# Output projection by Strassen's seven products, with the mixed heads stored in the forms the products use

## The chip, the cores and the metric

The kernel runs on one core of a Trainium2 chip. The core has five engines that run side by side, each through its own queue in order: TensorE (PE in the profile, with its weight loads as PEld), VectorE (DVE), ScalarE (ACT), GpSimd (POOL) and SyncE (SP, which here only issues DMAs). The metric is the device time of one execution in microseconds (us), taken as the median of several runs.

## The reference

One layer of a hybrid decoder, for 512 tokens and a model width of 2048, all in float32. A projection of the normalised and modulated input feeds a state space branch (SSD) and a retention branch. Their outputs, 2048 columns each, are laid side by side, and one output projection brings the 4096 columns back to 2048:

```
mixed = jnp.concatenate([y_ssd, y_ret], axis=-1) @ w_out[layer]
h = h + gate[:, None, :] * mixed
return rms_norm(h, final_norm_w)
```

The change concerns the product `@ w_out` (512 x 4096 by 4096 x 2048), what comes after it, and the place where the two branches hand over their outputs.

## The kernel before, in words

**Every float32 product is three products.** The matrices are split into a high part of reduced precision and the rest: ACT casts (`hi`, L96; `mh`, L655), DVE subtracts (`lo`, L97; `ml`, L656). `mm3` (L104 to L106) then issues high by high, high by low and low by high into the same bank of PSUM. One matmul has 128 rows of contraction, 128 output rows and 512 output columns.

**Input projection.** `unit` computes 512 columns at a time: for each of 8 steps `load_w` brings 256 rows of weights (512 KB) through SP into one of three buffers with the tag `raw`, splits them, and PE makes 24 matmuls. Units for the state space groups come first (`xs1` to `xs3`, `z1` to `z3`), then for each of four pairs of retention heads `qk`, `v` and `g`. Beside `v`, `gate_part` loads the weights of the residual gate through the same three `raw` buffers and multiplies them on DVE (L527, L529).

**Handover.** `ssd_b` and `ret_c` end in four calls of `put_mix(i, src, nw)`. It transposes a 512 x 128 block on PE, scales it on ACT into `m` (L331), and POOL sends it to DRAM as `mix[i]`, 128 features by 512 tokens (L332). There are 32 such blocks.

**Output projection.** For each of four blocks of 512 output columns there are 16 steps `kc`. A step reads two blocks `mix` (POOL's queue, L639, into the tag `xs`; blocks 12 to 31 are read once and stay in SBUF) and 256 rows of `w_out` (SP's queue), splits both, and makes 24 matmuls into four banks, one for each block of 128 tokens (tile `o`). Then for each of the four: times the gate (`h<-o,gate`, L680), plus the residual (L681), the squares' sum for the last norm on ACT (`jk`, L683), times the norm's weight (L686). In the last block of columns the four last steps are held back and PE takes them token block by token block, in an order written out by hand, so that a row of outputs can be finished and sent while PE works on the next (L689 to L699).

**Order.** The order of the instructions on each engine is set when the kernel is compiled: a planner runs through the program with costs of its own and puts each instruction where it thinks it ready, in the order of the program among equals. On the chip each queue then keeps that order, and an instruction that waits holds up all behind it on its engine. Buffers with the same tag take turns: the fourth `raw` waits until the first is free. `hi` and `lo` have four buffers each, `ul` (where `mh` and `ml` lie) has 17.

Of the kernel before, what the change touches and what calls it, by code (L numbers as in the profile page):

```python
# [41 lines left out]
def hybrid_block(ctx, tc, x, c_row, vecs, heads, w_mod, w_gate, b_gate, w_in, w_dt, w_out, fnw,  # L42
# [35 lines left out]
    # silu(c), halved conv taps and norm weights (the gates below carry a factor 2)  # L78
# [23 lines left out]
    def mm3(dst, a, b, first, last):  # L102
        (ah, al), (bh, bl) = a, b
        pe.matmul(dst, lhsT=ah, rhs=bh, start=first, stop=False)  # L104
        pe.matmul(dst, lhsT=ah, rhs=bl, start=False, stop=False)  # L105
        pe.matmul(dst, lhsT=al, rhs=bh, start=False, stop=last)  # L106
# [211 lines left out]
    mix = [dram.tile([P, L], F32, name=f"mix{i}") for i in range(32)]  # L318
# [6 lines left out]

    def put_mix(i, src, nw):
# [4 lines left out]
        act.activation(m, pT, AF.Copy, scale=nw)  # L331
        pool.dma_start(mix[i], m)  # L332

# [1 line left out]
    def ssd_a(g):  # L335
# [15 lines left out]
        for c in range(NC):  # L351
# [29 lines left out]
            if c < NC - 1:  # L381
                xw = t2k("xw", 1, "xw")
                pool.tensor_tensor(v8(xw), v8(xd), bcast_h(dte[:, c, hs]), ALU.mult)
                pst = bank("aux", "pst")
                pe.matmul(pst, lhsT=bn[:, sl], rhs=xw, start=True, stop=True)
                new = t2k("prev", 2, "new")
                if c == 0:
                    act.copy(new, pst)
                else:
                    pool.tensor_tensor(v8(new), v8(prev), bcast_h(cdec[:, c, hs]), ALU.mult)  # L390
                    dve.tensor_tensor(new, pst, new, ALU.add)
                prev = new
# [31 lines left out]
    def ret_a(p, qk):  # L424
        rr = [rotary(qk[i], f"r{i}") for i in range(4)]
        sts, kzs, qxs = [], [], []
        for j in range(2):
# [8 lines left out]
            for c in range(NC):  # L436
# [5 lines left out]
                              dmk[:, h, :].unsqueeze(1).to_broadcast([P, NC, P]), ALU.mult)  # L442
# [3 lines left out]
                               xib[:, h, :].unsqueeze(1).to_broadcast([P, NC - 1, P]), ALU.mult)  # L446
# [93 lines left out]
    dts = t2k("mo", 2, "dts")  # L540
# [52 lines left out]
    acsT = t2k("mo", 2, "acsT", (P, P))  # L593
# [36 lines left out]
    kept = {}  # L630

    def mix_tile(k):
        if k in kept:
            return kept[k]
        if k < RING:
            mr = t2k("xs", 5, "mr")
        else:
            kept[k] = mr = res.tile([P, L], F32, tag=f"mix{k}", name=f"mr{k}")
        pool.dma_start(mr, mix[k])  # L639
        return mr  # L640

    sso = const.tile([P, NC, 4], F32, name="sso")
    hout = [[None] * 4 for _ in range(NC)]
    for n in range(4):
        cols = slice(n * 512, (n + 1) * 512)
        banks = [bank("mm", f"o{t}") for t in range(NC)]
        fw = t2k("bc", 5, f"fw{n}")
        sp.dma_start(fw, fnw[cols].partition_broadcast(P))
        for kc in range(16):
            mh, ml = [], []  # L650
            for kt in range(2):
                mr = mix_tile(2 * kc + kt)
                mhk = up.tile([P, L], F32R, tag="ul", bufs=NK + 1, name="mh")
                mlk = up.tile([P, L], F32R, tag="ul", bufs=NK + 1, name="ml")
                act.copy(mhk, mr)  # L655
                dve.tensor_tensor(mlk, mr, mhk.bitcast(F32), ALU.subtract)  # L656
                mh.append(mhk)
                ml.append(mlk)
            hi, lo = load_w(w_out[16 * n + kc], 512)
            tail = n == 3 and kc >= 12  # L660
            if kc <= 12 or not tail:
                held = []
            held.append((kc, mh, ml, hi, lo))
            if tail and kc < 15:
                continue
            order = [(e, b, kt) for e in held for kt in range(2) for b in range(NC)]
            if tail:
                order = [(e, b, kt) for b in range(NC) for e in held for kt in range(2)]
            ctl = tc.manual_schedule(engines={pe.engine}) if tail else nullcontext()
            ctl.__enter__()  # L670
            for (kc_, mh_, ml_, hi_, lo_), b, kt in order:
                sl = slice(b * P, (b + 1) * P)
                mm3(banks[b], (mh_[kt][:, sl], ml_[kt][:, sl]), (hi_[:, kt, :], lo_[:, kt, :]),
                    kc_ == 0 and kt == 0, kc_ == 15 and kt == 1)
            ctl.__exit__(None, None, None)
        for t in range(NC):
            xr = t2k("zs", 4, "xr")
            sp.dma_start(xr, x[t * P:(t + 1) * P, cols])
            h = up.tile([P, 512], F32, tag="uh", bufs=NK, name=f"h{t}_{n}")
            dve.tensor_tensor(h, banks[t], gate[n], ALU.mult)  # L680
            dve.tensor_tensor(h, h, xr, ALU.add)  # L681
            jk = res.tile([P, 512], F32, tag="jk", bufs=2, name="jk")
            act.activation(jk, h, AF.Square, accum_out=sso[:, t, n:n + 1])  # L683
            hout[t][n] = h
            if n < 3:
                dve.tensor_tensor(h, h, fw, ALU.mult)  # L686
                continue
            rs = small.tile([P, 1], F32, name="rs")
            dve.tensor_reduce(rs, sso[:, t, :], mybir.AxisListType.X, ALU.add)  # L689
            rsqrt_into(rs, rs, 1.0 / D, EPS)  # L690
            for m in range(4):
                h = hout[t][m]
                if m == 3:
                    dve.scalar_tensor_tensor(h, h, rs, fw, ALU.mult, ALU.mult)
                elif m == 2:
                    dve.tensor_scalar(h, h, rs, None, ALU.mult)
                else:
                    act.activation(h, h, AF.Copy, scale=rs)
                (sp if m % 2 else act).dma_start(out[t * P:(t + 1) * P, m * 512:(m + 1) * 512], h)  # L699
# [74 lines left out]
```

## Time and profile before

| | |
|---|---|
| median of 3 runs | 1522.89 us (1522.87 to 1524.67) |
| span of the profiled execution, first to last instruction | 1520.7 us |
| what the median has beyond that span | 2.2 us |
| busy, share of the span: PE, DVE, ACT, POOL | 97%, 57%, 35%, 18% |
| output projection, first to last matmul | 1161.1 to 1510.9 us, 1536 matmuls |
| moved by DMA | 228.65 MB, 150 GB/s over the span |

The profiled execution's time is known by its span alone; it lies 2.2 us under the median, and the difference is what stands around the first and the last instruction. "Busy" is the time in which at least one instruction of the engine ran. Matmuls overlap in the pipeline, so PE's pace is read from the distance of their starts and not from the length of one. A row of the timeline gives start and length; where an instruction had to wait inside the engine, its length contains that wait.

### The profile page before, as it was taken

Reading aid. Unit: us, or ns where it says so; the run is one execution under the profiler, and the core shown is the slowest. Engines: PE = TensorE matmul, PEld = TensorE weight load, DVE = VectorE, ACT = ScalarE, POOL = GpSimd, SP = SyncE. Lnnn points to the kernel's source line nnn. Section 1 sums busy time; section 2 is a strip of 40 time slices with the busy share of each in tenths; the row PEclk is TensorE's granted clock in tenths of the full one; section 3 lists DMA queues with packets and bytes.
Section 4 is the critical chain, followed back from the end, with each engine's and each line's share of the span. In section 5 each row is a group of like instructions: output and inputs, shape, how many; then the busy total and the mean of one; then the engine's idle time right before and its main releaser. Section 6 shows DMA issues by size and latency. Waiting matters only on the chain.

```text
span 1520.7 us, 17260 instructions
## 1 busy us (share of the span) xinstructions
PE 1473.2 (97%) x6673; PEld 1205.0 (79%) x6673; DVE 861.4 (57%) x1080; ACT 531.4 (35%) x744; POOL 275.8 (18%) x326
## 2 busy tenths in 40 slices
PE   6998999999999999999999999999999999999997
PEld 4766888778888888788878887888788888888886
DVE  6899777774554563733364345435444455464644
ACT  6423443534323433122222221222223444444443
POOL 4540015360042041200020011002021310000000
PEclk9999999999999999999999999999999999999999
DMA  9888542434234224522452345234546754463523
GB/s 358 330 311 278 171 126 84 138 112 124 86 110 135 87 84 152 165 92 85 142 182 70 97 152 173 69 95 148 188 125 193 254 157 159 121 189 95 173 93 111
DMA packets 63060, 228.65 MB, mean 150 GB/s; under 512 B 7809, under 2 KB 7985, under 8 KB 58881
## 3 DMA queue, kind: packets, MB, share of 16 engines
q1 hardware_dynamic: 50834, 188.89, 38.5%
q0 software_dynamic: 10992, 36.56, 7.1%
q10 hardware_dynamic: 1152, 2.10, 0.4%
q8 instruction: 52, 0.85, 0.2%
q14 instruction: 30, 0.25, 0.0%
HBM read 214.87 MB, written 12.65 MB: 150 GB/s over the span
## 4 chain that ended last, share of the span: by engine, by line
PE 69%; DVE 6%; DMA 5%; POOL 2%; issue 1%; ACT 1%; ACTq 0%; POOLq 0%; DVEq 0%
PE acc L105 14%; PE acc L106 14%; PE acc L104 14%; PE o L106 8%; PE o L104 8%; PE o L105 8%; DMA graw<-w_gate_d 4%; DVE lo L97 2%; PE py L372 1%; PE po L466 1%; PE pT L329 1%; DVE gacc L529 1%; PE po L468 1%; PE pkv L487 1%; POOL r L421 1%
## 5 line engine op out<-in xcount | busy, mean ns | idle before, releaser
L97 DVE TENSOR_TENSOR lo<-raw,hi 128x1024 fp32r<-128x1024 f32 x230 | 285.8, 1244 | 295.9 <-ACT hi L96 295.4
L96 ACT CAST hi<-raw 128x1024 fp32r<-128x1024 f32 x248 | 254.0, 1027 | 564.1 <-PE acc L106 241.9
L104 PE MATMUL acc<-hi,uh 128*128 128x512 f32 x704 | 274.6, 393 | 6.6 <-DVE rt L420 6.3
L105 PE MATMUL acc<-lo,uh 128*128 128x512 f32 x704 | 278.7, 396 | 0.0
L106 PE MATMUL acc<-hi,ul 128*128 128x512 f32 x704 | 276.4, 393 | 0.0
L106 PE MATMUL acc<-uh,lo 128*128 128x512 f32 x512 | 200.9, 393 | 0.0
L105 PE MATMUL acc<-ul,hi 128*128 128x512 f32 x512 | 200.6, 392 | 0.0
L104 PE MATMUL acc<-uh,hi 128*128 128x512 f32 x512 | 200.4, 393 | 0.0
L104 PE MATMUL o<-hi,mh 128*128 128x512 f32 x512 | 199.4, 389 | 0.0
L105 PE MATMUL o<-lo,mh 128*128 128x512 f32 x512 | 199.3, 389 | 0.0
L106 PE MATMUL o<-hi,ml 128*128 128x512 f32 x512 | 197.7, 389 | 0.0
L104 PEld LDWEIGHTS acc<-hi,uh 128*128 128x128 f32 x704 | 132.2, 188 | 35.2 <-DVE rt L420 7.5
L656 DVE TENSOR_TENSOR ml<-mr,mh 128x512 fp32r<-128x512 f32 x128 | 88.4, 692 | 125.5 <-PE o L105 98.1
L106 PEld LDWEIGHTS acc<-hi,ul 128*128 128x128 f32 x704 | 132.3, 188 | 27.4 <-issue 0.5
L105 PEld LDWEIGHTS acc<-lo,uh 128*128 128x128 f32 x704 | 132.3, 188 | 27.2 <-issue 0.5
L105 PEld LDWEIGHTS acc<-ul,hi 128*128 128x128 f32 x512 | 96.6, 189 | 19.8
L104 PEld LDWEIGHTS acc<-uh,hi 128*128 128x128 f32 x512 | 96.6, 189 | 19.5
L106 PEld LDWEIGHTS acc<-uh,lo 128*128 128x128 f32 x512 | 96.5, 188 | 19.7
L105 PEld LDWEIGHTS o<-lo,mh 128*128 128x128 f32 x512 | 96.1, 188 | 20.0
L106 PEld LDWEIGHTS o<-hi,ml 128*128 128x128 f32 x512 | 96.1, 188 | 19.9
L104 PEld LDWEIGHTS o<-hi,mh 128*128 128x128 f32 x512 | 96.1, 188 | 19.7
L655 ACT CAST mh<-mr 128x512 fp32r<-128x512 f32 x128 | 79.1, 619 | 70.2 <-PE o L106 62.9
(220 smaller groups left out, 1668.5 us busy)
## 6 DMA issues: line engine op xcount, KB each, us to landing
ada<-w_mod_d SPq DMA_DIRECT2D x32, 1024.0 KB, 5.8
raw<-w_out_d SPq DMA_DIRECT2D x64, 512.0 KB, 3.7
mr<-mix POOLq DMA_DIRECT2D x68, 256.0 KB, 3.8
raw<-w_in_z SPq DMA_DIRECT2D x32, 512.0 KB, 3.6
raw<-w_in_qk SPq DMA_DIRECT2D x32, 512.0 KB, 3.6
raw<-w_in_v SPq DMA_DIRECT2D x32, 512.0 KB, 3.8
graw<-w_gate_d SPq DMA_DIRECT2D x32, 512.0 KB, 4.2
raw<-w_in_g SPq DMA_DIRECT2D x32, 512.0 KB, 3.6
```

Of the source, the lines that this page charges most:

```text
L96: act.copy(hi, raw)
L97: eng.tensor_tensor(lo, raw, hi.bitcast(F32), ALU.subtract)
L104: pe.matmul(dst, lhsT=ah, rhs=bh, start=first, stop=False)
L105: pe.matmul(dst, lhsT=ah, rhs=bl, start=False, stop=False)
L106: pe.matmul(dst, lhsT=al, rhs=bh, start=False, stop=last)
L329: pe.transpose(pT[:, c * P:(c + 1) * P], src[c], ident)
L372: pe.matmul(py[:, hd], lhsT=dec[:, h, :], rhs=xd[:, hd], start=True, stop=True)
L421: pool.tensor_tensor(r, r, t, ALU.add)
L466: pe.matmul(po[:, e], lhsT=sts[j][:, sl], rhs=vs[c][:, e], start=True, stop=c == 0)
L468: pe.matmul(po[:, e], lhsT=qxs[j][:, sl], rhs=prev[:, e], start=False, stop=True)
L655: act.copy(mhk, mr)
L656: dve.tensor_tensor(mlk, mr, mhk.bitcast(F32), ALU.subtract)
```

## The change

The product is cut into 2 x 2 x 2 blocks: two of 256 tokens, two in the contraction (even and odd blocks of 128 features), and two of 512 columns, twice over (`q` = 0, 1, for 1024 output columns each). In place of the eight products of blocks, seven products of sums of blocks are made (Winograd's form of Strassen's scheme).

The sums on the side of the mixed heads are made once, in `put_mix`: of two successive blocks `m`, POOL makes four sums of 128 x 256 and sends five pieces to DRAM (`AS`, `SR`, `S2`, `A12`, `A22`; 896 KB for the two, before 512 KB). The sums on the side of the weights are made in the output projection, on POOL, from reordered weights (`_quads`). Each `q` has three loops over eight `jj`:

- first loop, two steps `e` for each `jj`: products into the banks `Y`, `W` and `Z`; on POOL two sums of 128 x 512 per step (`raw`, `t2`);
- second loop, for each `jj`: the sum `t2` is carried on twice and two further sums are made on POOL, products into `Y`, `Z` and `W`;
- third loop: the carried sums `t2` by `A22` into the banks `X`.

Between the first and the second loop `Y`, `Z` and `W` are copied out or added up (`e1`, `u2`, `w1`) while their banks go on accumulating; after the second they are combined and finished. The hand-written order of PE is dropped; in the last loop three `jj` are held back instead.

With that some things move: the mixed heads are read through SP's queue (no longer POOL's), all 32 blocks' forms for each `q` (28.7 MB, before 17.4 MB); `w_out` is read in pieces of 512 and 256 KB (50 MB in all, before 33.5 MB); the norm's weights `fw` come through POOL's queue; the retention tables `dmk` and `xib` are loaded for each pair of heads by POOL and not once; `mo` has 3 buffers and `xw` 2, `jk` 1.

```diff
-    mix = [dram.tile([P, L], F32, name=f"mix{i}") for i in range(32)]
+    QJ = 8
+    mixd = {f: [dram.tile([P, 2, 256], F32, name=f"mix{f}{j}") for j in range(n)]
+            for f, n in (("AS", 2 * QJ), ("SR", 2 * QJ), ("S2", QJ), ("A12", QJ), ("A22", QJ))}
...
-        m = t2k("mo", 2, "m")
+        m = t2k("mo", 3, "m")
         act.activation(m, pT, AF.Copy, scale=nw)
-        pool.dma_start(mix[i], m)
+        if i % 2 == 0:
+            half_of["m"] = m
+            return
+        ma, j = half_of["m"], i // 2
+        a11, a21, a12, a22 = ma[:, 0:256], ma[:, 256:], m[:, 0:256], m[:, 256:]
+        g = t2k("xw", 2, "mg", (P, 2, 256))
+        s2 = t2k("xd", 2, "ms", (P, 256))
+        pool.tensor_tensor(g[:, 0, :], a11, a21, ALU.subtract)
+        pool.tensor_tensor(a21, a21, a22, ALU.subtract)
+        pool.tensor_tensor(s2, a21, a11, ALU.subtract)
+        pool.tensor_tensor(g[:, 1, :], a12, s2, ALU.add)
+        pool.dma_start(mixd["AS"][j].rearrange("p a t -> p (a t)"), ma)
+        pool.dma_start(mixd["SR"][j], g)
+        pool.dma_start(mixd["S2"][j // 2][:, j % 2, :], s2)
+        pool.dma_start(mixd["A12"][j // 2][:, j % 2, :], a12)
+        pool.dma_start(mixd["A22"][j // 2][:, j % 2, :], a22)
...
+    def finish(t, n, c, more=None):
+        xr = t2k("zs", 4, "xr")
+        sp.dma_start(xr, x[t * P:(t + 1) * P, n * 512:(n + 1) * 512])
+        h = res.tile([P, 512], F32, tag="h", bufs=16, name=f"h{t}_{n}")
+        if more is not None:
+            dve.tensor_tensor(h, c, more, ALU.add)
+            c = h
+        dve.tensor_tensor(h, c, gate[n], ALU.mult)
+        dve.tensor_tensor(h, h, xr, ALU.add)
+        jk = res.tile([P, 512], F32, tag="jk", bufs=1, name="jk")
+        act.activation(jk, h, AF.Square, accum_out=sso[:, t, n:n + 1])
...
+    def split(dst, src, eng=dve):
+        act.copy(dst[0], src)
+        eng.tensor_tensor(dst[1], src, dst[0].bitcast(F32), ALU.subtract)
...
+    def mul(banks, m, i, w, k, first, last, rows=(0, 1), more=False):
+        for t in rows:
+            sl = slice(i * 256 + t * P, i * 256 + (t + 1) * P)
+            mm3(banks[t], (m[0][:, sl], m[1][:, sl]), (w[0][:, k, :], w[1][:, k, :]), first, last, more)
...
+        for jj in range(QJ):
+            ms2 = m_pair(mixd["S2"][jj])
+            t2w = w_pair()
+            for e in range(2):
+                first, last = jj == e == 0, jj == QJ - 1 and e == 1
+                t2 = up.tile([P, 512], F32, tag="uh", bufs=NK, name="t2")
+                sp.dma_start(t2, w_out[QJ * q + jj][:, (5 if e else 2) * 512:(6 if e else 3) * 512])
+                raw = w_raw(q, jj, 6 * e)
+                m = m_pair(mixd["AS"][2 * jj + e])
+                pool.tensor_tensor(raw[:, 1 - e, :], raw[:, 0, :], raw[:, 1, :], ALU.add)
+                w = w_pair()
+                split(w, raw)
+                mul(by, m, 0, w, e, first, last)
+                mul(bw, m, 1, w, 1 - e, first, last)
+                pool.tensor_tensor(t2, t2, raw[:, 1 - e, :], ALU.add)
+                split([v[:, e, :] for v in t2w], t2)
+                mul(bz, ms2, e, t2w, e, first, last)
+                t2s.append(t2)
...
+        for jj in range(QJ):
+            raw = w_raw(q, jj, 3)
+            m = m_pair(mixd["A12"][jj])
+            w = w_pair()
+            split(w, raw)
+            for e in range(2):
+                t2 = t2s[2 * jj + e]
+                pool.tensor_tensor(t2, t2, raw[:, e, :], ALU.add)
+                mul(by, m, e, w, e, False, jj == QJ - 1 and e == 1, more=True)
+            for e in range(2):
+                last = jj == QJ - 1 and e == 1
+                raw = w_raw(q, jj, 5 if e else 1)
+                m = m_pair(mixd["SR"][2 * jj + e])
+                pool.tensor_tensor(raw[:, e, :], raw[:, 0, :], raw[:, 1, :], ALU.add)
+                w = w_pair()
+                split(w, raw)
+                mul(bz, m, 0, w, e, False, last, more=True)
+                mul(bw, m, 1, w, 1 - e, False, last, more=True)
+        for t in range(2):
+            finish(t, n0, by[t])
+        for t in range(2):
+            dve.tensor_tensor(e1[t], bz[t], e1[t], ALU.add)
+            dve.tensor_tensor(u2[t], bw[t], u2[t], ALU.subtract)
+            pool.tensor_tensor(w1[t], w1[t], e1[t], ALU.subtract)
+            finish(t, n1, u2[t])
+            finish(2 + t, n1, w1[t])
...
+        for jj in range(QJ):
+            m = m_pair(mixd["A22"][jj])
+            w = w_pair()
+            for e in range(2):
+                split([v[:, e, :] for v in w], t2s[2 * jj + e])
+            held.append((jj, m, w))
+            if q and QJ - 3 <= jj < QJ - 1:
                 continue
...
+            for t in range(2):
+                for jj_, m, w in held:
+                    for e in range(2):
+                        mul(bx, m, e, w, e, jj_ == e == 0, jj_ == QJ - 1 and e == 1, (t,))
```

`m_pair` reads a form through SP into the tag `xs` and splits it (ACT cast, DVE subtraction) into the tag `ul`; `w_raw` reads 128 x 1024 weights into `raw`; `w_pair` takes a pair of `hi` and `lo`. `weighted` and `store` are the last norm's steps of before.

More of the change, by code (lines that the diff above doesn't have):

```diff
@@ L100, in hybrid_block, with mm3 @@
     uh, ul = [], []
-    def mm3(dst, a, b, first, last):
+    def mm3(dst, a, b, first, last, more=False):
         (ah, al), (bh, bl) = a, b
-        pe.matmul(dst, lhsT=ah, rhs=bh, start=first, stop=False)
-        pe.matmul(dst, lhsT=ah, rhs=bl, start=False, stop=False)
-        pe.matmul(dst, lhsT=al, rhs=bh, start=False, stop=last)
+        pe.matmul(dst, lhsT=ah, rhs=bh, start=first, stop=False, skip_group_check=more)
+        pe.matmul(dst, lhsT=ah, rhs=bl, start=False, stop=False, skip_group_check=more)
+        pe.matmul(dst, lhsT=al, rhs=bh, start=False, stop=last, skip_group_check=more)
     def unit(name, w_stationary, tag="mm", side=None):
@@ L426, in ret_a @@
         sts, kzs, qxs = [], [], []
+        dmk, xib = (att.tile([P, 2, P], F32, tag=tg, bufs=2, name=tg) for tg in ("dmk", "xib"))
+        pool.dma_start(dmk, dmask[:, 2 * p:2 * p + 2, :])
+        pool.dma_start(xib, xi[2 * p:2 * p + 2, :].partition_broadcast(P))
         for j in range(2):
@@ L629, in hybrid_block @@
     res = ctx.enter_context(tc.tile_pool(name="res", bufs=1))
[L630 to L640, printed above, removed]
+    fws = []
+    for n in range(4):
+        fw = res.tile([P, 512], F32, tag=f"fw{n}", name=f"fw{n}")
+        pool.dma_start(fw, fnw[n * 512:(n + 1) * 512].partition_broadcast(P))
+        fws.append(fw)
@@ L642, in hybrid_block @@
     sso = const.tile([P, NC, 4], F32, name="sso")
     hout = [[None] * 4 for _ in range(NC)]
[L644 to L664, printed above, removed]
-                continue
[L666 to L699, printed above, removed]
@@ new lines, in weighted, with store @@
+    def weighted(t, n):
+        dve.tensor_tensor(hout[t][n], hout[t][n], fws[n], ALU.mult)
+    def store(t, late):
+        rs = small.tile([P, 1], F32, name="rs")
+        dve.tensor_reduce(rs, sso[:, t, :], mybir.AxisListType.X, ALU.add)
+        rsqrt_into(rs, rs, 1.0 / D, EPS)
+        for m in [late] + [m for m in range(4) if m != late]:
+            h = hout[t][m]
+            if m == late:
+                dve.scalar_tensor_tensor(h, h, rs, fws[m], ALU.mult, ALU.mult)
+            elif m == late ^ 1:
+                dve.tensor_scalar(h, h, rs, None, ALU.mult)
+            else:
+                act.activation(h, h, AF.Copy, scale=rs)
+            (sp if m % 2 else act).dma_start(out[t * P:(t + 1) * P, m * 512:(m + 1) * 512], h)
@@ new lines, in split, with w_raw, w_pair, m_pair @@
+    def split(dst, src, eng=dve):
+        act.copy(dst[0], src)
+        eng.tensor_tensor(dst[1], src, dst[0].bitcast(F32), ALU.subtract)
+    def w_raw(q, jj, at):
+        raw = wp.tile([P, 2, 512], F32, tag="raw", bufs=3, name="raw")
+        sp.dma_start(raw.rearrange("p k f -> p (k f)"),
+                     w_out[QJ * q + jj][:, at * 512:(at + 2) * 512])
+        return raw
+    def w_pair():
+        return [wp.tile([P, 2, 512], F32R, tag=tg, bufs=4, name=tg) for tg in ("hi", "lo")]
+    def m_pair(src):
+        mr = t2k("xs", 5, "mr")
+        sp.dma_start(mr, src.rearrange("p a t -> p (a t)"))
+        mh = up.tile([P, 512], F32R, tag="ul", bufs=NK + 1, name="mh")
+        ml = up.tile([P, 512], F32R, tag="ul", bufs=NK + 1, name="ml")
+        split((mh, ml), mr)
+        return mh, ml
@@ L724, in _blocks, with _quads @@
     return w.reshape(-1, P, rows // P * cols)
+def _quads(w):
+    k, n = w.shape
+    b = w.reshape(k // 512, 2, 2, P, n // 1024, 2, 512).transpose(4, 0, 3, 1, 2, 5, 6)
+    order = [(0, 0, 0), (0, 0, 1), (0, 1, 1), (0, 1, 0), (1, 1, 0), (1, 1, 1), (1, 0, 1), (1, 0, 0)]
+    return np.stack([b[:, :, :, e, i, j] for e, i, j in order], axis=3).reshape(-1, P, 8 * 512)
 IN_UNITS = {"BC0": ((COL_B, 256), (COL_C, 256)), "xs0a": ((COL_XS, 256),), "z0": ((COL_Z, 512),),
@@ L755 @@
         "w_dt_d": a["w_in"][0][:, COL_DT:COL_Q].reshape(NK, P, HEADS).transpose(1, 0, 2),
-        "w_out_d": _blocks(a["w_out"][0], 256, 512),
+        "w_out_d": _quads(a["w_out"][0]),
         "fnw_d": a["final_norm_w"],
```

45 lines of the change are left out of this document (36 added, 9 removed).

## The prediction

> **What bounds the kernel now.** I read the page's head first, then the stage in the table of stretches, then the groups by line, last the timeline where two engines meet.
>
> ```profile
> span 1520.7 us, 17260 instructions
> PE 1473.2 (97%) x6673; PEld 1205.0 (79%) x6673; DVE 861.4 (57%) x1080; ACT 531.4 (35%) x744; POOL 275.8 (18%) x326
> PEclk9999999999999999999999999999999999999999
> PE 69%; DVE 6%; DMA 5%; POOL 2%; issue 1%; ACT 1%; ACTq 0%; POOLq 0%; DVEq 0%
> ```
>
> PE is busy nearly throughout, at full granted clock, and 69% of the chain that ended last is its. In the stage that changes (first the matmuls into `o` alone, then all engines):
>
> ```profile
> core 0: us, PE busy (x) PEld busy (x) DVE busy (x), PEclk, DMA share, GB/s
> 1161.00:1511.00 350.00, 349.26 (x1536) 288.17 (x1536) 10.31 (x16) 1.00 0.48 154
> core 0: us, PE busy (x) PEld busy (x) DVE busy (x) ACT busy (x) POOL busy (x), PEclk, DMA share, GB/s
> 1161.00:1511.00 350.00, 349.95 (x1552) 289.59 (x1550) 189.31 (x237) 149.93 (x223) 34.40 (x66) 1.00 0.48 154
> ```
>
> 1536 matmuls without a hole: about 349.7 us, 0.2277 us each. DVE has 189 us of work in that time, POOL 34 us, nearly all of it issuing DMAs. So PE alone bounds this stage, and there is room on DVE and POOL, if the two may run beside each other.
>
> **The gain on PE.** The loops of the new scheme make 48 + 48 + 16 calls of `mul` for each `q`, each 2 x 3 matmuls: 672, so 1344 for both in place of 1536, of the same shape. 192 x 0.2277 = 43.7 us less. By phase and `q`: 65.6 us of PE in the first loop (16 steps of 18), 65.6 in the second (8 of 36), 21.9 in the third (96).
>
> **What the sums cost.** The durations:
>
> ```profile
> L97 DVE TENSOR_TENSOR lo<-raw,hi 128x1024 fp32r<-128x1024 f32 x230 | 285.8, 1244 | 295.9 <-ACT hi L96 295.4
> L96 ACT CAST hi<-raw 128x1024 fp32r<-128x1024 f32 x248 | 254.0, 1027 | 564.1 <-PE acc L106 241.9 <-PE acc L105 184.2 <-PE o L106 107.1
> L656 DVE TENSOR_TENSOR ml<-mr,mh 128x512 fp32r<-128x512 f32 x128 | 88.4, 692 | 125.5 <-PE o L105 98.1 <-PE acc L106 11.3 <-issue 6.8
> L655 ACT CAST mh<-mr 128x512 fp32r<-128x512 f32 x128 | 79.1, 619 | 70.2 <-PE o L106 62.9 <-DMA mr<-mix 6.9
> 324.77 1.29 POOL L378 TENSOR_TENSOR xc<-xc,y 128x512 f32<-128x512 f32 x1 [1.71 <-DVE y L377]
> 1160.84 1.22 DVE L97 TENSOR_TENSOR lo<-raw,hi 128x1024 fp32r<-128x1024 f32 x1
> 1161.97 0.68 DVE L656 TENSOR_TENSOR ml<-mr,mh 128x512 fp32r<-128x512 f32 x1
> 1162.58 0.68 DVE L400 SCALAR_TENSOR_TENSOR gs<-th,acc 128x512 f32<-128x512 f32 x1
> ```
>
> Back to back, DVE needs 1.13 us for 1024 columns and 0.61 for 512 (distance of starts). A POOL sum of two plain 512-wide operands takes 1.29 us alone. Each engine by itself would fit: in a step of the first loop (4.10 us of PE) DVE has half an `S2`, an `AS`, a `raw` and a `t2` to subtract: 0.30 + 0.61 + 1.13 + 0.61 = 2.65; ACT 0.31 + 0.62 + 1.03 + 0.62 = 2.58; POOL two sums, 2.58. The question is whether DVE's and POOL's fit together. The timeline, in two places where they meet:
>
> ```profile
> 772.35 1.23 DVE L97 TENSOR_TENSOR lo<-raw,hi 128x1024 fp32r<-128x1024 f32 x1
> 772.40 2.31 POOL L421 TENSOR_TENSOR r<-r,rt 128x512 f32<-128x512 f32 x1 [3.17 <-DVE rt L420]
> 548.64 1.04 POOL L383 TENSOR_TENSOR xw<-xd,dte 128x512 f32<-128x512 f32 x1
> 548.71 2.06 DVE L357 TENSOR_TENSOR dec<-dec,acs 128x1024 f32<-128x1024 f32 x1 [1.50 <-POOL dec L355]
> 549.65 2.02 POOL L368 TENSOR_TENSOR xc<-xc,dsk 128x512 f32<-128x512 f32 x1
> 550.69 2.06 DVE L97 TENSOR_TENSOR lo<-raw,hi 128x1024 fp32r<-128x1024 f32 x1
> 552.67 1.21 DVE L360 TENSOR_TENSOR dec<-dec,cbt 128x1024 f32<-128x1024 f32 x1
> 546.45 1.03 POOL L390 TENSOR_TENSOR new<-new,cdec 128x512 f32<-128x512 f32 x1
> 546.51 0.69 DVE L379 TENSOR_TENSOR y<-py,xc 128x512 f32<-128x512 f32 x1 [0.28 <-POOL xc L378]
> ```
>
> At 772 POOL's sum starts beside DVE's `lo`, lasts 2.31 us and ends 1.13 us after `lo` does: it ran when `lo` was done. At 548 four instructions alternate; each that starts second lasts twice as long, and all four need 4.11 us (548.64 to 552.75), the sum of their single runs. At 546 the two run side by side unharmed: there one of DVE's operands (`py`) lies in PSUM. So a DVE instruction with both operands in SBUF and a POOL sum exclude each other. Every subtraction of `split` is of that kind, and every new sum on POOL. Their times add up:
>
> - First loop, a step: 2.65 + two sums at 1.18 (between 1.13, queued behind DVE, and 1.24 or 1.29 alone; nearer the queued one, since it will be) = 5.0, against 4.10 of PE. 16 steps: 80.2 per `q`, against 65.6.
> - Second loop, a `jj`: three pairs of subtractions, 3 x (1.13 + 0.61) = 5.22, and four sums, 4.72: 9.94, against 8.20. 8 of them: 79.5, against 65.6.
> - Third loop and the finishing: 24 subtractions 14.6; 24 operations on results at 0.69 (L680 below) 16.6; two sums on POOL 2.4; norm weights and scaling some 4.9. Together 38.5, against PE's 21.9. ACT has 1.86 per `jj` here and is covered.
>
> That is 198 us per `q`, 396 for both. Off go 5 us for a step that is made ready before the stage (two of four `hi`/`lo` pairs are free then), 4 for what lies behind the last matmul and is counted in the tail, 3 for finishing that reads PSUM and lets POOL run: 384, against 349.7 now: **+34.7 us** where PE would give -43.7.
>
> The ends: with every instruction hidden behind its neighbour as at 548 (1.08 for 1024, 0.56 for 512, 1.13 on POOL) a step is 4.74 and a `jj` 9.44; stage 364, +14.5. With the full single durations (1.23, 0.69, 1.29) they are 5.53 and 10.92; stage 424, +74. I take the middle value since POOL puts two sums between three and a half subtractions: some are hidden, some not.
>
> The Trainium skill ("SBUF — State Buffer", section "Who interferes with whom") says that DVE and GpSimd share a pair of SBUF ports under an exclusive lock, taken among others by a DVE instruction with two SBUF inputs against a GpSimd one that reads SBUF: who starts first has it for the whole instruction, and the other blocks. Taken literally with whole durations that is the upper end, 424 us; this trace agrees on the exclusion, but its alternating run at 548 (4.11 us for what is 1.04, 1.04, 1.23 and 1.23 alone, 4.54) shows less than whole durations.
>
> **The other steps.**
>
> ```profile
> DMA  9888542434234224522452345234546754463523
> GB/s 358 330 311 278 171 126 84 138 112 124 86 110 135 87 84 152 165 92 85 142 182 70 97 152 173 69 95 148 188 125 193 254 157 159 121 189 95 173 93 111
> mr<-mix POOLq DMA_DIRECT2D x68, 256.0 KB, 3.8
> raw<-w_out_d SPq DMA_DIRECT2D x64, 512.0 KB, 3.7
> 596.82 0.33 SPq L518 DMA_DIRECT2D graw<-w_gate_d  x1
> 604.04 0.33 SPq L518 DMA_DIRECT2D graw<-w_gate_d  x1
> 292.44 0.54 POOL L332 DMA_DIRECT2D mix<-m  x1 [4.99 <-ACT m L331]
> 293.55 0.54 POOL L332 DMA_DIRECT2D mix<-m  x1 [0.57 <-ACT m L331]
> 297.69 1.04 POOL L383 TENSOR_TENSOR xw<-xd,dte 128x512 f32<-128x512 f32 x1 [3.59 <-DVE xd L365]
> 1510.56 0.39 PE L106 MATMUL o<-hi,ml 128*128 128x512 f32 x1
> 1510.99 0.69 DVE L680 TENSOR_TENSOR h<-o,gate 128x512 f32<-128x512 f32 x1 [0.99 <-PE o L106]
> 1511.71 0.69 DVE L681 TENSOR_TENSOR h<-h,xr 128x512 f32<-128x512 f32 x1
> ```
>
> *Traffic.* A step of the first loop reads 1.15 MB, a `jj` 2.3 MB: some 230 GB/s at the pace above. The first slices moved 358 GB/s, so it is covered; without that cover a step would last 3.2 us at 358, still under PE. On SP a step issues 3.5 DMAs at 0.33 us. A `raw` that waits for its buffer holds up the `m` issued behind it, and with it ACT, DVE and PE; this is priced as a rival.
>
> *Handover.* For two blocks POOL gets four sums of 256 columns (about half of 1.29 each, 2.6 us) and five DMA issues in place of two (+1.6 us). Queued behind are the POOL steps of the next group, as `xw` at 297.69. In front of it stand 3.59 us idle and as much between the stores, against 8.4 us for a group's two pairs. At best it costs nothing, since each later group has a unit of 192 matmuls (44 us) between store and next use; at worst 4 us here and a slowed `lo` or two. I take +1.
>
> *Tables.* `dmk` and `xib` are loaded per pair: eight small POOL issues, 0.54 each, waiting on nothing but their buffer; hidden behind the `qk` unit. If they came late, `st` on DVE would wait, and the unit `v` (44 us of PE) covers it.
>
> *Copies between the loops.* PE's first products with `A12` wait for `e1`, two ACT copies; but `W` and `Z` of the last step (12 matmuls, 2.7 us) stand between, and PE has slack anyway. Nothing.
>
> *Tail.* From the last matmul (1510.56) to the end of the span are 10.1 us. The last block has one more DVE operation (+0.7); the last token blocks come one behind the other as before.
>
> Sum: +34.7 + 1 + 0.7 = +36. The profiled span of 1520.7 stands 2.2 us under the median, and the difference stays: 1522.9 + 36 = **1559 us**.
>
> **The rivals.**
>
> *Faster: the sums run beside DVE after all.* Then PE keeps the stage, and 1522.9 - 43.7 + 1.7 = 1481. For it: DVE is idle for 161 of the 350 us now, and the unharmed meeting at 546. Against it: the meetings of SBUF operands at 548 and 772. It decides if a step's joint time falls under 4.10 us, that is if POOL's 2.36 us fit over half beside DVE's.
>
> *Slower still: the ring of three `raw` buffers.* Beside `v` two loads through it are 7.22 us apart (596.82 to 604.04 is one round of two), 3.61 us per load or a life of 10.8 us for a buffer. Here POOL's sum (1.18) comes between landing and cast: 12.0 us, 4.0 per load. The second loop needs 24: 96 us in place of 79.5, twice, +33: 1592. Against it: beside `v` the loads also waited in DVE's queue behind `gacc`, and a life of landing 3.7, sum 1.18, cast 1.03 and subtraction 1.13 with a wait of 1 at each would be 10.0, just the 3.3 per load that the joint time allows.
>
> *About as before.* Best packing of DVE and POOL (+14.5) and much of the finishing beneath PE: within 0.2% (3 us, about what a measurement of this kernel tells from no change), 1523.
>
> **How the numbers follow.** Forecast (joint time of DVE and POOL, its own range 1538 to 1599 by the two ends) 0.69; ring of `raw` 0.16; faster 0.12; as before 0.03. Slower by over 0.2% is 0.69 + 0.16 = 0.85, faster 0.12, same 0.03. The range leaves out the faster case, the same, and what the ring could add beyond 1600: 1528 to 1600, some 0.81.
>
> **What would show it.** In the stretch of the output projection PE should be about 80% busy, with its waits ended by DVE subtractions; the sums on POOL should last 1.8 to 2.3 us in the mean and the subtractions clearly over 0.69 and 1.23; a step of the first loop 5.0 us, a `jj` of the second 9.9; 1344 matmuls. Wrong would be: sums near 1.29 with PE at 99% (then it is faster); PE's waits ended by DMAs into `raw` (ring); a hole at the start of the stage, where sums on POOL stand behind the last stores of the heads.

## The result and the profile after

| | before | after |
|---|---|---|
| median | 1523.39 us (1522.87 to 1524.67, 4 runs) | 1535.55 us (1534.36 to 1538.24, 4 runs) |
| span of the profiled execution | 1520.7 us | 1532.6 us |
| matmuls of the output projection | 1536 | 1344 |
| first of them starts, last of them starts | 1161.1, 1510.56 | 1146.69, 1516.41 |

The ratio is 1.0086, with a 95% interval of 1.007 to 1.0103: slower by 12.2 us where 36 were forecast. The page of the changed kernel, head and groups (a row gives line, engine, operation, out<-in, count, busy time, mean ns of one, and the idle time just before with what ended it):

```profile
PE 1448.2 (94%) x6481; PEld 1169.3 (76%) x6481; DVE 1035.2 (68%) x1160; ACT 570.6 (37%) x816; POOL 546.8 (36%) x512
PE 60%; DVE 12%; DMA 4%; POOL 4%; issue 3%; ACT 2%; POOLq 0%; DVEq 0%; ACTq 0%; SPq 0%
L700 DVE TENSOR_TENSOR lo<-raw,hi 128x1024 fp32r<-128x1024 f32 x80 | 146.1, 1827 | 14.5 <-ACT hi L699 14.3
L700 DVE TENSOR_TENSOR ml<-mr,mh 128x512 fp32r<-128x512 f32 x112 | 122.7, 1097 | 17.8 <-PE acc L107 11.2
L743 POOL TENSOR_TENSOR raw<-raw 128x512 f32<-128x512 f32 x32 | 54.7, 1710 | 82.1 <-DMA raw<-w_out_d 47.8
```

PE works 25 us less over the span, and the chain that ended last holds 60% of PE and 12% of DVE, before 69% and 6%. The same subtractions that took 1.23 and 0.69 us take 1.83 and 1.10, and a sum of two plain 512-wide operands takes 1.71. Now the stage by its loops: the first two loops of `q` = 0, its third loop up to the first matmul of `q` = 1, the first two loops of `q` = 1, its third loop, and what lies behind the last matmul. (The products into `X` of the third loop of `q` = 0 run on beside those of `q` = 1, until 1335.5.)

```profile
core 0: us, PE busy (x) PEld busy (x) DVE busy (x) ACT busy (x) POOL busy (x), PEclk, DMA share, GB/s
1146.70:1303.50 156.80, 140.75 (x592) 108.33 (x590) 144.66 (x107) 78.62 (x113) 113.15 (x80) 0.99 0.73 237
1303.50:1329.20 25.70, 21.27 (x75) 14.84 (x73) 25.70 (x33) 12.71 (x26) 10.78 (x7) 0.87 0.64 201
1329.20:1493.70 164.50, 144.98 (x599) 113.25 (x599) 153.32 (x132) 82.88 (x123) 100.95 (x58) 0.97 0.68 213
1493.70:1516.60 22.90, 22.16 (x98) 17.82 (x96) 22.28 (x39) 12.61 (x27) 7.36 (x6) 1.00 0.15 47
1516.60:1532.60 16.00, 0.20 (x1) 0.00 (x0) 7.36 (x14) 5.49 (x11) 2.43 (x5) 0.66 0.72 263
```

DVE is busy for 92 to 100% of every stretch ahead of the last matmul, PE for 83 to 97%. PE's waits in the stage (us in total, times, longest) end with DVE's subtractions nearly every time, once with the copy of a bank between the loops, and once for long with a cast on ACT:

```profile
PE Y L106 <- DVE lo L700: 18.7, 20, 2.6
PE Z L106 <- DVE lo L700: 6.3, 9, 1.0
PE Y L105 <- ACT e L754: 5.9, 1, 5.9
PE X L106 <- DVE lo L700: 5.1, 4, 2.9
PE Y L105 <- ACT hi L699: 4.2, 1, 4.2
```

The holes cost more than their own length. Four times in the stage the granted clock falls to 0.5 for 3.4 to 6.9 us, each time in or just behind a longer wait of PE (2.6 to 5.9 us), as here around the one for the copy of `Y` into `e1` (the last line is a stretch, with the columns of the table above):

```profile
1421.86 0.80 PE L105 MATMUL Y<-hi,mh 128*128 128x512 f32 x1 [5.87 <-ACT e L754]
1422.46 0.63 PE L106 MATMUL Y<-lo,mh 128*128 128x512 f32 x1
1422.88 0.63 PE L107 MATMUL Y<-hi,ml 128*128 128x512 f32 x1
1419.30:1426.00 6.70, 4.14 (x10) 3.28 (x11) 4.78 (x5) 4.97 (x8) 4.33 (x4) 0.50 0.85 292
```

Matmuls there start 0.43 us apart in place of 0.23; 34 of them together are some 7 us of PE's time (an estimate: 34 times 0.2). The stage before has no such spell.

And the meeting itself, in the second loop:

```profile
1256.45 1.75 POOL L770 TENSOR_TENSOR raw<-raw 128x512 f32<-128x512 f32 x1 [1.08 <-DVE lo L700]
1256.37 0.68 DVE L700 TENSOR_TENSOR ml<-mr,mh 128x512 fp32r<-128x512 f32 x1
1256.98 2.31 DVE L700 TENSOR_TENSOR lo<-raw,hi 128x1024 fp32r<-128x1024 f32 x1
1259.21 0.68 DVE L700 TENSOR_TENSOR ml<-mr,mh 128x512 fp32r<-128x512 f32 x1
```

POOL's sum starts during `ml` and lasts 0.46 us longer than the 1.29 it takes alone; the `lo` that comes to wait behind it lasts 2.31 in place of 1.23.

**Where the 11.9 us of the spans come from:** the stage starts 14.4 us earlier, lasts 20.2 us longer (349.5 to 369.7 between the starts of its first and last matmul), and the tail is 6.1 us longer (10.1 to 16.2 from the start of the last matmul): -14.4 + 20.2 + 6.1 = +11.9.

### The profile page after: what moved, and what is told of

It is laid out like the page before. It is cut to its first block, busy times and chain, and to the rows that moved or that the text cites. A ratio compares the mean times of both kernels' runs of the same rounds, so it can differ in the third digit from the quotient of the medians.

```text
span 1532.6 us, 17621 instructions
## 1 busy us (share of the span) xinstructions
PE 1448.2 (94%) x6481; PEld 1169.3 (76%) x6481; DVE 1035.2 (68%) x1160; ACT 570.6 (37%) x816; POOL 546.8 (36%) x512
## 4 chain that ended last, share of the span: by engine, by line
PE 60%; DVE 12%; DMA 4%; POOL 4%; issue 3%; ACT 2%; POOLq 0%; DVEq 0%; ACTq 0%; SPq 0%
PE acc L105 16%; PE acc L107 16%; PE acc L106 16%; DVE lo L700 6%; DMA raw<-w_out_d 4%; DVE ml L700 2%; POOL raw L770 1%; PE py L390 1%; PE po L487 1%; ACT hi L699 1%; PE pT L332 1%; PE Y L106 1%; PE po L489 1%; PE pkv L508 1%; POOL t L764 1%
## 5 line engine op out<-in xcount | busy, mean ns | idle before, releaser
L97 DVE TENSOR_TENSOR lo<-raw,hi 128x1024 fp32r<-128x1024 f32 (+1 forms) x166 | 211.4, 1276 | 256.0 <-ACT hi L96 253.3
L96 ACT CAST hi<-raw 128x1024 fp32r<-128x1024 f32 (+1 forms) x184 | 186.4, 1017 | 440.9 <-PE acc L107 193.8
L700 DVE TENSOR_TENSOR lo<-raw,hi 128x1024 fp32r<-128x1024 f32 x80 | 146.1, 1827 | 14.5 <-ACT hi L699 14.3
L700 DVE TENSOR_TENSOR ml<-mr,mh 128x512 fp32r<-128x512 f32 x112 | 122.7, 1097 | 17.8 <-PE acc L107 11.2
L699 ACT CAST hi<-raw 128x1024 fp32r<-128x1024 f32 x80 | 84.0, 1050 | 104.3 <-POOL raw L770 68.4
L187 DVE SCALAR_TENSOR_TENSOR ada<-ada,csb 128x2048 f32<-128x2048 f32 x32 | 90.9, 2843 | 0.3 <-DMA ada<-w_mod_d 0.3
L550 DVE SCALAR_TENSOR_TENSOR gacc<-graw,cs,gacc 128x512 f32<-128x512 f32 x60 | 50.4, 841 | 57.2 <-DMA graw<-w_gate_d 56.1
L743 POOL TENSOR_TENSOR raw<-raw 128x512 f32<-128x512 f32 x32 | 54.7, 1710 | 82.1 <-DMA raw<-w_out_d 47.8
L75 POOL TENSOR_SCALAR mv<-mv 128x2 f32<-128x2 f32 x16 | 3.1, 191 | 204.6 <-DVE mv L496 204.6
L699 ACT CAST mh<-mr 128x512 fp32r<-128x512 f32 x112 | 68.4, 616 | 17.5 <-PE W L107 13.2
```

What stands on the lines that cost most here:

```text
L96: act.copy(hi, raw)
L97: eng.tensor_tensor(lo, raw, hi.bitcast(F32), ALU.subtract)
L550: dve.scalar_tensor_tensor(gacc, raw[:, kk, :], cs[:, k:k + 1], gacc, ALU.mult, ALU.add)
L699: act.copy(dst[0], src)
L700: eng.tensor_tensor(dst[1], src, dst[0].bitcast(F32), ALU.subtract)
L743: pool.tensor_tensor(raw[:, 1 - e, :], raw[:, 0, :], raw[:, 1, :], ALU.add)
```

## Experiments

Theory: in the stage DVE's subtractions and POOL's sums exclude each other, and their joint time sets its length. Rivals: the ring of three `raw` buffers, or POOL's place in the chain from load to cast. Open besides: what brings the stage forward by 14.4 us, and what lengthens the tail. The kernel before, run beside them, had medians of 1521.12 to 1522.2 us.

### Without the sums, and with sums that read nothing

```diff
 no_sums:
-                pool.tensor_tensor(raw[:, 1 - e, :], raw[:, 0, :], raw[:, 1, :], ALU.add)
 (and so the three other sums of the two loops)
 memset:
-                pool.tensor_tensor(raw[:, 1 - e, :], raw[:, 0, :], raw[:, 1, :], ALU.add)
+                pool.memset(raw, 0.0)
 (and so the three others; t2 where the sum goes into t2)
```

> Leaves out the four kinds of sums on the weights' side in the output projection (POOL, 128 tensor_tensor of 128x512); everything else as in the changed kernel, so its output is not the layer's. Shared port (theory): DVE alone then needs 2.65 us per step of the first loop and 5.22 per jj of the second, under PE's 4.10 and 8.20; both loops of a q take 131 us, not the 157 to 159 measured; total 1535.6 - 53 = about 1482 us, subtractions back at 0.69 and 1.23. Ring of three raw buffers (rival): a buffer's life loses only the sum of 1.2 to 1.8 us, 24 loads at 3.6 us in the second loop still take 86 us: about 1505 us, with PE waiting for DMAs into raw.

> Each sum on POOL is replaced by a memset of the same buffer (raw: 1024 columns, t2: 512), so POOL still has an instruction at the same place in its queue, with the same waits before and behind it, but reads nothing from SBUF; the output is not the layer's. Shared port for reads (theory): the subtractions on DVE are not blocked, 0.69 and 1.23 us; near the run without sums, 1482 to 1492 us. Queue and latency (rival: the time is lost because cast and subtraction wait behind one more instruction in the chain from DMA to PE): near the changed kernel, 1520 to 1536 us.

Without sums: 1470.75 us, ratio 0.9672 (0.9658 to 0.9686). With memsets in their place: 1474.79 us, ratio 0.9695 (0.9681 to 0.971). Both lie on the theory's side and below its figures (1482, and 1482 to 1492). The stage of each, first `no_sums`, then `memset`:

```profile
1147.30:1454.50 307.20, 306.54 (x1359) 253.27 (x1356) 240.57 (x309) 189.20 (x290) 27.86 (x30) 1.00 0.78 259
```

```profile
1146.30:1457.40 311.10, 307.74 (x1358) 252.87 (x1357) 238.76 (x306) 185.33 (x288) 108.79 (x140) 1.00 0.77 253
L770 POOL MEMSET raw<- 128x1024 f32 x32 | 30.6, 955 | 109.9 <-DMA raw<-w_out_d 105.1
L700 DVE TENSOR_TENSOR lo<-raw,hi 128x1024 fp32r<-128x1024 f32 x80 | 99.1, 1239 | 52.4 <-ACT hi L699 52.3
```

In the second kernel POOL has an instruction in the same place of the same chain, 0.96 us long into `raw` and 0.53 into `t2`, and the same DMAs, queues and buffers. `lo` is back at 1.24 us and PE is busy for 307.7 of 311.1 us. So neither the ring of `raw` nor one more engine between load and cast, busy for so long, costs more than 4 us; about 61 of the 65 us that the sums cost go when POOL no longer reads operands. A memset is also shorter than a sum (1.29 us alone), and how much of the 61 us that makes was not separated; the length of DVE's subtractions doesn't hang on it. The Trainium skill ("SBUF — State Buffer", section "Who interferes with whom") says that a DVE instruction with two SBUF inputs contends with a GpSimd instruction that reads SBUF, and not with one that only writes it. These two runs agree: 1827 ns beside sums, 1239 beside memsets, 1244 beside nothing.

### The sums on DVE

```diff
-                pool.tensor_tensor(raw[:, 1 - e, :], raw[:, 0, :], raw[:, 1, :], ALU.add)
+                dve.tensor_tensor(raw[:, 1 - e, :], raw[:, 0, :], raw[:, 1, :], ALU.add)
 (and so the three others)
```

> The same sums on DVE in place of POOL, full result. Shared port (theory): a sum costs 0.61 us on DVE where it took 1.18 of the joint time on POOL; a step 2.65 + 1.22 = 3.87 us against PE's 4.10, a jj 5.22 + 2.44 = 7.66 against 8.20: the loops become PE's again, finishing stays DVE's; about 1488 us (1478 to 1500). Rival (POOL did carry work that DVE has no room for): DVE, busy 346 of 370 us in the stage already, gets 128 x 0.69 = 88 us more and the kernel gets slower, 1560 us or more.

1514.92 us, ratio 0.9952 (0.9934 to 0.9971): all the work on one engine is 20 us faster than shared between two, since a sum costs 0.69 us there, not 1.71 and a longer subtraction. It is still slower than expected, by 15 us or more:

```profile
1148.40:1495.80 347.40, 318.69 (x1359) 254.69 (x1356) 308.37 (x427) 188.43 (x288) 23.37 (x30) 0.99 0.70 226
1157.79 0.69 DVE L743 TENSOR_TENSOR raw<-raw 128x512 f32<-128x512 f32 x1 [4.63 <-DMA raw<-w_out_d]
1161.93 0.80 PE L106 MATMUL Z<-lo,mh 128*128 128x512 f32 x1 [4.65 <-DVE lo L700]
L770 DVE TENSOR_TENSOR raw<-raw 128x512 f32<-128x512 f32 x32 | 22.1, 689 | 22.6 <-DMA raw<-w_out_d 22.6
```

DVE now waits for loads itself, with all its other work queued behind: 4.6 us at the start of the stage, 22.6 us in the second loops, in front of the sums into `raw`. No engine is full (PE 319, DVE 308 of 347): with POOL out of the way the ring of `raw` seems to come next.

### More buffers

```diff
 ring (and from the ninth load on alone: ring_late)
-        raw = wp.tile([P, 2, 512], F32, tag="raw", bufs=3, name="raw")
+        turn[0] += 1
+        raw = (res.tile([P, 2, 512], F32, tag="raw5", bufs=2, name="raw") if turn[0] % 5 > 2 else
+               wp.tile([P, 2, 512], F32, tag="raw", bufs=3, name="raw"))
```

> The changed kernel with five raw buffers in the output projection in place of three. Theory (joint time of DVE's subtractions and POOL's sums): little, 1528 to 1536; PE's stage stays 362 to 370 us, and the waits of POOL's raw for DMA shrink while those of ACT's hi for POOL stay. Rival (the ring of three buffers held the loads back after all): stage 345 to 350 us, 1510 to 1516.

> The changed kernel with five raw buffers from the ninth load on, so that the two new ones are asked for only after the retention tiles in whose place they lie are free (in the run ring, the first of them held up SP's queue and PE for 22 us). Theory (joint time of DVE and POOL): a jj of the second loop stays 9.5 to 9.8 us, 1532 to 1537. Rival (the ring): a jj goes to 8.2 to 8.8, 1518 to 1526.

`ring`: 1546.64 us, ratio 1.0159 (1.0146 to 1.0172), outside both expectations; `ring_late`: 1538.24, ratio 1.0117 (1.0096 to 1.0137), just above the theory's. Both have a hole on PE early in the stage, first `ring`, then `ring_late`:

```profile
1179.80 1.22 PE L105 MATMUL Y<-hi,mh 128*128 128x512 f32 x2 [21.92 <-ACT hi L699]
```

```profile
1198.11 1.64 POOL L654 DMA_DIRECT2D fw<-fnw_d  x3 [2.48 <-issue]
1199.82 1.26 POOL L747 TENSOR_TENSOR raw<-raw 128x512 f32<-128x512 f32 x1
1202.20 1.22 PE L105 MATMUL Y<-hi,mh 128*128 128x512 f32 x2 [13.05 <-ACT hi L699]
```

In `ring` the new buffers lie where the retention tiles lay, so the first load into them waits on SP until the last mixed forms are stored, and every load behind it too. In `ring_late` a sum stands on POOL behind the last stores and the loads of `fw`: the hole that the prediction feared at the handover, called up by another order. The holes spoil the totals; the pace of the second loop does not suffer from them (distance of starts of matmuls into `Y`, one `jj` apart, in us):

```
after        q=0: 9.2 10.1 9.7 9.5 9.8 9.8 9.7    q=1: 10.2 8.2 8.2 8.2 8.5 9.4 9.6    mean 9.3
ring_late    q=0: 8.2 8.4 10.7 8.5 10.6 9.7 9.5   q=1: 8.6 8.9 9.6 9.5 9.7 8.5 10.7    mean 9.4
no_sums      q=0: 8.3, then 8.2                   q=1: 8.3, then 8.2                   mean 8.2
```

With five buffers 9.4 us as with three: the ring is not what bounds the changed kernel.

### The tail

```diff
+            ctl = tc.manual_schedule(engines={pe.engine}) if q and jj == QJ - 1 else nullcontext()
+            ctl.__enter__()
             for t in range(2):
                 for jj_, m, w in held:
                     for e in range(2):
                         mul(bx, m, e, w, e, jj_ == e == 0, jj_ == QJ - 1 and e == 1, (t,))
+            ctl.__exit__(None, None, None)
```

> The changed kernel with PE's last products in the written order: 18 matmuls of the first token block, then 18 of the second, as the kernel before ends. Theory (the tail is 5.9 us longer since both blocks come ready together): 1531 to 1533, tail 12 to 14 us in place of 16.0. Rival (DVE's backlog of finishing, not the order, sets the end): 1535, tail 16.

1536.52 us, ratio 1.0091 (1.0076 to 1.0105): no difference from the changed kernel in the medians. In its profiled execution the tail is 13.4 us, 2.8 less, but the stage 2.3 us longer. The rows of the changed kernel show what the end is like: DVE comes to the last two results together, 1.6 us after the last matmul has started, and finishes them in step.

```profile
1516.41 0.39 PE L107 MATMUL X<-hi,ml 128*128 128x512 f32 x1
1517.97 1.28 DVE L665 TENSOR_TENSOR h<-X,e 128x512 f32<-128x512 f32 x2
1519.17 1.28 DVE L667 TENSOR_TENSOR h<-h,gate 128x512 f32<-128x512 f32 x2
1520.37 1.28 DVE L668 TENSOR_TENSOR h<-h,xr 128x512 f32<-128x512 f32 x2
```

So the rival holds for the total; that the order of PE is worth some 3 us of the tail was seen in one execution and not in the time.

### What brings the stage forward

Four variants of the kernel before, its old output projection kept. `b_forms` has the whole handover of the change (tables per pair, buffers, sums and five stores) beside the old store; `b_tables_mo3` only tables and buffers; `b_stores` the five stores without the sums (plain halves are sent); `b_sums` the sums without the stores. In all but `b_tables_mo3` blocks are handled two at a time, as in the change.

```diff
 b_tables_mo3
-        m = t2k("mo", 2, "m")
+        m = t2k("mo", 3, "m")
...
+        dmk, xib = (att.tile([P, 2, P], F32, tag=tg, bufs=2, name=tg) for tg in ("dmk", "xib"))
+        pool.dma_start(dmk, dmask[:, 2 * p:2 * p + 2, :])
 b_stores has besides, b_sums not
+        pool.dma_start(mixd["AS"][j].rearrange("p a t -> p (a t)"), ma)
+        (four more)
 b_sums has besides, b_stores not
+        pool.tensor_tensor(g[:, 0, :], a11, a21, ALU.subtract)
+        (three more)
```

> The kernel before with the change's handover alone: put_mix makes the sums and stores the five pieces beside the old block (which the old output projection reads), tables loaded per pair, mo with 3 and xw with 2 buffers. Theory for the 14.4 us by which the stages ahead of the output projection got shorter: the handover's POOL instructions shift the planner's clock, and it puts DVE's rotary steps, subtractions and gate steps beside qk and v in another order, without PE's waits there: about 1523.4 - 14 = 1509 us. Rival (the gain belongs to the new output projection): 1523 us, or 1524 to 1528 with 9 us more of POOL per group.

> The kernel before with two parts of the change alone: dmk and xib loaded per pair, and a buffer more for mo and xw. Theory (the 14.4 us ahead of the output projection come from the new sums and stores of the mixed forms, which move DVE's rotary steps ahead in the order): no effect, 1520 to 1523, first matmul into o near 1161, PE still waiting at psc -> acc (1.8 us) and acc -> pk (1.1 us) in each pair. Rival (the tables' place or the buffers free something): those waits go, first matmul into o at 1148 to 1152, 1508 to 1512.

> The kernel before with per-pair tables, the buffers for mo and xw and the five stores of the mixed forms beside the old store, but none of the four sums (the stores send plain halves instead; nothing reads them). Its DVE order has the rotary steps early, as the changed kernel has. Theory (the order DVE is given makes the upstream gain): first matmul into o at 1149 to 1151, 1512 to 1517. Rival (the POOL sums at the handover make it, by whatever way): 1160 to 1163, 1521 to 1525.

> The same, but with the four POOL sums and none of the five stores (the sums are used by nothing). Its DVE order is that of the kernel before. Theory (order): first matmul into o at 1160 to 1163, 1521 to 1525, PE waiting again at psc -> acc and acc -> pk in each pair. Rival (the sums make the gain): 1149 to 1151, 1512 to 1517.

The order of DVE's instructions in the second pair of heads, as the programs have it (G residual gate, l a subtraction of weights, R rotary, S scores' mask), with what was measured:

```
                                                  first matmul   median    ratio to before (95%)
before        GGlGGlGlGRRGRGlRlGGSlSGG...          1161.1
b_tables_mo3  GGlGGlGlGRRGRGlRlGGSGSGll...         1161.6        1524.86   1.0018 (1.0008 to 1.0029)
b_sums        GGlGGlGlGRRGRGlRlGGSGSGll...         1169.3        1525.72   1.0031 (1.0015 to 1.0048)
b_stores      GGlGlGlGRGRRGlRGlGSGSlGG...          1149.3        1516.01   0.9963 (0.9949 to 0.9977)
b_forms       GGlGlGlGRGRRGlRGlGSGSlGG...          1149.9        1516.01   0.9962 (0.9947 to 0.9978)
after         GGlGlGlGRGRRGlRGlGSGSlGG...          1146.7
```

Not all of this was expected. Tables and buffers alone were to cost nothing and cost 2.9 us; the whole handover was to give 14 us and gave 5.1, although its stage starts 11.2 us earlier; `b_sums` lies a little above what the theory gave, in both numbers. The profiled execution of `b_sums` was a slower one of its nine (1530.62 us against a median of 1525.72), so 1169.3 is some us high.

With the new order PE's waits go. In the stretch from 600 to 1150 us, first before, then `b_sums`, then `b_stores` (in the changed kernel there are none):

```profile
PE acc L104 <- DVE rt L420: 6.3, 5, 1.7
PE pk L432 <- POOL r L421: 3.2, 5, 0.7
```

```profile
PE acc L104 <- DVE rt L435: 6.9, 7, 1.6
PE pk L450 <- POOL r L436: 5.3, 6, 1.6
```

```profile
PE pk L449 <- POOL r L435: 1.8, 3, 1.0
PE acc L104 <- DVE rt L434: 0.3, 1, 0.3
```

The rotary steps of a pair begin one gate step earlier where the five stores stand in the program, and not where the sums, tables or buffers do. Two kernels with the old order start the stage at or after 1161 us, two with the new at 1149 to 1150. Tables, buffers and sums together cost 3 to 4 us by the median of `b_sums`, about the upper end that the prediction gave the handover; most of that is there without the sums (2.9 us in `b_tables_mo3`). Stores and order come together in these runs, and the order alone wasn't tried; but that more stores on POOL's queue should make PE wait less by any other way, nothing in the traces suggests. Nor is the order of the pairs the whole: of the 14.4 us 2.4 are there by the last matmul into `po` of the state space groups (561.8 us before, 559.4 after). They too come with the stores (558.8 and 559.2 us in `b_stores` and `b_forms`, 561.8 and 565.0 in the two others). The other 12 arise in the four pairs of heads, and some 3 of the 14.4 no variant reproduces. `b_stores` and `b_forms` lose part of it at the very end, where 3.2 us pass between the drain of SP and the next step of POOL in the closing sequence; the changed kernel doesn't show that, and its cause is open.

### Towards a better version

```diff
 sums_dve_qt: sums_dve, the order of tail, and
-                sp.dma_start(t2, w_out[QJ * q + jj][:, (5 if e else 2) * 512:(6 if e else 3) * 512])
+                pool.dma_start(t2, w_out[QJ * q + jj][:, (5 if e else 2) * 512:(6 if e else 3) * 512])
-        sp.dma_start(xr, x[t * P:(t + 1) * P, n * 512:(n + 1) * 512])
+        pool.dma_start(xr, x[t * P:(t + 1) * P, n * 512:(n + 1) * 512])
 best: sums_dve, the order of tail, the buffers of ring_late, and in the first loop
-                dve.tensor_tensor(t2, t2, raw[:, 1 - e, :], ALU.add)
+                (pool if q == 0 and jj < 2 else dve).tensor_tensor(t2, t2, raw[:, 1 - e, :], ALU.add)
 (and so the sum into raw)
```

> Sums on DVE (1514.9 us by itself), with the loads of t2 and xr issued by POOL, whose queue is then nearly idle, in place of SP, and PE's last products in the written order. Theory (a raw load issued late on SP behind t and xr loads makes the hole of some 10 us at the start of the stage, and the tail's order costs 2 to 4): first 36 matmuls without a hole, 1500 to 1506. Rival (the hole is the landing of the loads themselves, all of them together): hole stays, 1511 to 1515.

> Sums on DVE, except on POOL for the first four steps of the first q (where DVE stood behind a sum whose load was late, 7 us of PE idle), five raw buffers from the ninth load on, and PE's last products in the written order. Theory (with POOL out of the way the ring of three is the next limit: a jj of the second loop took 8.9 to 9.5 us with DVE only 83% busy): a jj at 8.2 to 8.4, no hole at the start, 1494 to 1502. Rival (DVE's own work is the limit, or the order of its instructions): jj 8.9 or more, 1505 to 1512.

`sums_dve_qt`: 1511.05 us, ratio 0.9923 (0.9907 to 0.9939). The hole stays, so the queue of t2 and xr was not its cause; the rival holds. It shows the next limit: a `jj` takes 9.0 us in the mean, with DVE busy for 83% of the stretch from 1230 to 1290. `best`: **1491.16 us, ratio 0.9811 (0.979 to 0.9833)**, faster than expected.

```profile
1147.10:1476.00 328.90, 314.37 (x1359) 256.46 (x1357) 308.63 (x430) 189.75 (x290) 26.73 (x30) 0.98 0.73 240
L774 DVE TENSOR_TENSOR raw<-raw 128x512 f32<-128x512 f32 x32 | 21.8, 682 | 2.5 <-DMA raw<-w_out_d 2.3
```

DVE's idle time in front of the second loop's sums, 22.6 us in `sums_dve`, falls to 2.5, a `jj` to 7.9 in the mean (most at PE's own 8.2; a distance is shorter where the order of products into `Y` differs from one `jj` to the next), and the stage from 347.4 us to 328.9. Sixteen `jj` at 9.0 less 7.9 are 18 us: the ring, which did nothing beside sums on POOL, is by this worth most of the 20 us between `sums_dve_qt` and `best`. The two differ in the queue of t2 and xr and in the four first steps on POOL as well, which were not tried by themselves; PE's waits of 4.65 us for `lo` at the start have become 2.4, and 6.5 us of waiting for a cast in the first loop are left.

## Why the prediction was right in direction and wrong in size

The direction rested on the right mechanism; of the forecast's terms three failed, two by some 15 and 21 us and one by 5. That the time lies inside the stated range, near its lower end, is luck as far as those terms go.

- **Right: the joint time.** For `q` = 0 the first loop takes 79.4 us and the second 77.4, against 80.2 and 79.5 by the sum (together 156.8, against 159.7 less the 5 for a step made ready ahead); a `jj` of the second loop takes 9.2 to 10.1, against 9.94. Sums without reads give the time back (1474.79). For `q` = 1 the agreement is poorer: the first loop takes 92.7 us, with finishing of `q` = 0 beside it, and the second 71.9, with four `jj` at PE's own 8.2 to 8.5, after a hole of 5.9 us in which DVE made three pairs of subtractions while PE stood. Whole durations, the upper end (424 us for the stage, measured 369.7), are out. Added again from their own figures the two ends of the stage lie a few us further in than 364 and 424, which changes nothing. The signs named beforehand came: PE waits for DVE's subtractions, 1.83 and 1.10 us each. The sums, at 1.68 to 1.78 in the mean, are a little shorter than the 1.8 to 2.3 given, and PE was 89% busy, not 80%.
- **Wrong: the handover.** "I take +1" was -14.4. The trace of before showed the waits that went (`acc` for `rt`, 6.3 us, and `pk` for `r`, 3.2), but the prediction costed the handover with the order of all other instructions fixed. The planner orders anew: with five stores in one place the rotary steps stand earlier in another, and the stage starts 11.2 us earlier when only the handover is changed (`b_forms`). With the old order kept and no stores (`b_sums`) the step is worth +3 to +4, inside the +4 that was written as the worst. This is 15 of the 24 us between forecast and result; that it is the order itself and not the stores by another way is argued, not shown.
- **Wrong, the largest single term: third loop and finishing, 38.5 us per `q`.** They took 25.7 and 22.9 of the stage, the second at PE's own pace (22.16 of 22.9 busy). The sum laid all finishing end to end behind the second loop; in fact results of `q` = 0 are finished beside the loops of `q` = 1 (which take 164.5, not 159.7), and those of `q` = 1 partly behind the last matmul. Third loops as forecast 77 less the 7 taken off for tail and PSUM, in fact 48.6: -21; loops +7 (the hole and the half clock are in that); so the stage came out 14.5 us shorter than forecast.
- **Wrong: the tail.** +0.7 was forecast and +6.1 measured. "The last token blocks come one behind the other as before" is what failed: both blocks are finished in pairs from 1517.97 on, and DVE is busy with little break up to there (22.28 of 22.9 us in the third loop). The written order took 2.8 off in one profile and nothing off the median; how the rest divides is open.
- **Small: the copies between the loops**, costed at nothing, made one stall of 5.9 us, in `q` = 1. What failed is "`W` and `Z` of the last step (12 matmuls, 2.7 us) stand between": the products into `Z` came first there, and only four into `W` stood behind the last into `Y` (1414.70). The copies themselves stood in ACT's queue behind two casts that waited for POOL's sums:

```profile
1414.62 1.05 ACT L699 CAST hi<-raw 128x1024 fp32r<-128x1024 f32 x1 [4.32 <-POOL raw L770]
1419.76 1.04 ACT L699 CAST hi<-raw 128x1024 fp32r<-128x1024 f32 x1 [3.58 <-POOL raw L770]
1421.23 1.06 ACT L754 COPY e<-Y 128x512 f32<-128x512 f32 x2
```

- **Not in the sum: the clock.** All terms took the pace of full clock. The four spells at half clock are, by the estimate above, some 7 us of PE's time; how much of it DVE's pace hides was not measured.
- **The rivals.** The ring (0.16) falls for this kernel: five buffers leave the pace at 9.4 us. It was right about the next bound only. Sums running beside DVE (0.12) falls with the subtractions' 1.83 us beside sums and 1.24 beside memsets. "As before" (0.03) had one half right: much of the finishing did lie beside PE's work.

## What to carry to other kernels

Before giving an idle engine elementwise work, look in the trace for a place where the two engines run with the same kinds of operands; if they exclude each other, add their times, and compare with putting all of it on one (here 0.69 us for a sum on DVE, against 1.7 on POOL and 0.4 to 0.6 lost on a subtraction). When a bound is taken away, test the resource behind it again: five buffers were worth nothing with the first bound in place and, as far as `best` shows, most of 20 us without it. Where a planner orders the instructions, an edit in one stage can move another: compare the order of the engines' instructions in both programs before costing a step at nothing.

## What was not expected of the hardware

- POOL's memset of 128 x 1024 takes 955 ns and leaves DVE's subtractions at 1239 ns; POOL's sum of half that output takes 1710 ns there and brings them to 1827. What counts is the reading.
- A subtraction and a sum that meet do not lose a whole instruction each time: with 128 sums on POOL, 1.29 us each when alone, `lo` grew by 0.6 us and `ml` by 0.4 in the mean, and the sums by 0.4 to 0.5.
